# A decoder kernel on one Trainium2 core: two fetch pointers for the expert tiles, gates multiplied in before the next tile, a sum moved from GpSimd to VectorE, and one comparison instruction for two

## The chip, the cores and the metric

The kernel runs on one core of one Trainium2 chip. The core's engines are TensorE (PE in the profile, its weight loads PEld), VectorE (DVE), ScalarE (ACT), GpSimd (POOL) and SyncE (SP), which here only issues DMA transfers; 16 DMA engines move data between HBM and the on-chip memory. The metric is the device time of one execution in microseconds. A difference of about 0.3% (5 us here) is what a measurement of this kernel can tell from no change.

## The reference, cut to what matters

Two layers over 256 positions of 1024 features. Each layer is an attention (latent attention in layer 0, a sparse one in layer 1) followed by a feed-forward part of 16,384 small experts, "PEER", of which every token takes 16 for each of 8 heads. The change lies in that second part:

```python
def chunk(xc):                                     # 128 tokens
    q = (xc @ w_q).reshape(128, 8, 2, 128)
    sc = jnp.einsum("thpd,hpnd->thpn", q, subkeys)
    s_half, i_half = lax.top_k(sc, 16)             # per half, of 128 keys
    cand = s_half[:, :, 0, :, None] + s_half[:, :, 1, None, :]
    best, pos = lax.top_k(cand.reshape(128, 8, 256), 16)
    experts = ...                                  # i * 128 + j of the 16 best pairs
    g = jax.nn.softmax(best, axis=-1)
    a = gelu(einsum("thkd,td->thk", u[experts], xc))
    return einsum("thk,thkd->td", g * a, v[experts])
```

u and v are two tables of 16,384 rows of 1024 floats, 64 MB each per layer.

## The kernel before, in words

**Dense instead of gathered.** For 192 of the 256 tokens (`ND`) the kernel takes no rows by index. It streams the whole of u through TensorE as 128 tiles of 128 experts x 1024 (512 KB each), which gives every expert's dot product with every token; applies gelu; multiplies by a gate matrix that is zero where a token didn't choose the expert; and multiplies the result with the 128 tiles of v. The other 64 tokens are served by gathered rows: GpSimd fetches rows of u and v by index, and VectorE does the dot products (`g_dot`, L525) and the weighted sums (L537).

**The stages of a layer.** Attention; 16 tiles of the routing projection `p_wq` with the scores and the top-16 searches on VectorE; the u tiles (`u_step`); the v tiles. In the profiled execution the u tiles run from 178 to 541 us in layer 0 and from 1064 to 1430 us in layer 1.

**Split and plain tiles.** All weights are one list, `self.stream`, fetched in order by SP. A split tile comes into one of four places (`raw`). ScalarE rounds it to `hi` (L146), VectorE computes `lo = raw - hi` (L160), and `u_step` multiplies both with the activations, which are held as `hT` in the same two parts: 16 matmuls of `hi` and `lo` against them. Of each layer's 128 u tiles 75 are plain (`natural(j)`: every second one up to tile 44, two of three from there, none of the last four). They need neither ScalarE nor VectorE: they are loaded as `nat` and multiplied as full float32 with `xF`, the sum of the two parts of the activations, which L543 computes on GpSimd as the peer part begins.

**The fetch order.** `_sdma` (from L103) walks the list with one pointer, `sd`. A split tile is issued if it is no further than `_ahead()` says (as many split tiles as there are places); a plain one if it is at most `LEADN` = 4 tiles ahead of the tile in use, else the walk stops there, and what follows in the list waits too. `_slo` calls it after each `lo`, `end()` after each tile's matmuls. SP runs its queue in order: a `nat` transfer waits until TensorE is done with the tile that held its buffer, a `raw` one until its place is free. `nxt()` hands out the next tile: `prep()` (the `lo` of this tile, two `hi` ahead, the next `lo`), then `tick()`, which runs the functions put off by `defer(n, ...)`, n tiles later.

**The gates.** `final_gen` leaves, per token, the indices (`selI`) and the gates (`selG`) of its choices. For a group of 4 tokens (the quad, 48 of them per layer) `g_gen` has VectorE compare the indices against a ramp, once for each index part (L676, L677: 512 elements each, float16, so each choice becomes a one-hot row), and multiply one of the two by the gates in two parts (L678, L679). When two quads lie ready, `g_flush(2)` issues 8 one-hot matmuls for each (`acc<-hot`), which leave in PSUM the gate of every expert for 4 tokens. For slots of `A` that gelu has already filled, VectorE multiplies the gates in (L702); into the others ScalarE copies them (L704).

**The loop over the u tiles** (from L835) for tile j: `u_step(j)`, the matmuls; `u_fin` of tile j-1, which multiplies the gelu of the tile before it into its slot (L794), adds the two halves of a split tile (L803) and starts its gelu on ScalarE (L805, L808); `g_flush(2)`; `run_side`, which spends a budget of 0.8 (`GB`, in estimated us) on VectorE's side work, among it `g_gen`; and the dot products of gathered rows that are due. The engines take their instructions in the order in which they are written.

**After the last u tile** `w_start` turns the first slots into the weights `W` of the v stage (L819, L824), and the v tiles follow in the same list, as pairs of 1 MB.

Of the kernel before, what the change touches and what calls it, by code (L numbers as in the profile page):

```python
# [12 lines left out]
F32 = mybir.dt.float32  # L13
F32R = mybir.dt.float32r
BF16 = mybir.dt.bfloat16
F16 = mybir.dt.float16
# [31 lines left out]
class Kern:  # L48
# [5 lines left out]
    def plan(self):  # L54
        I, L = self.I, []
        self.v0s, self.spare, self.pairs = [], None, {}
        self.nh, self.odd, self.nat, self.natural = 0, {}, set(), {}
        if "mla" in self.parts:
            L += [I["a_w_in"][k] for k in range(KC)]
            L += [I["a_wk"][i] for i in range(2)]  # L60
            L += [I["a_wq"][i] for i in range(3)]
            L += [I["a_wv"][i] for i in range(2)]
            L += [I["a_wq"][i] for i in range(3, 6)]
            L += [I["a_wo"][i] for i in range(KC)]
        for l in (0, 1):
            if l == 1 and "nsa" in self.parts:
                L += [I["s_wv"][i] for i in range(4)]
                L += [I["s_wT"][i] for i in range(4)]
                L += [I["b_wg"]]
                L += [I["s_wT"][i] for i in range(4, 8)]  # L70
                L += [I["b_wq"][i] for i in range(4)]
                L += [I["b_wq"][i] for i in range(4, 8)]
                L += [I["b_wo"][i] for i in range(KC)] + [I["b_wo"][i] for i in range(KC // 2)]
            if f"peer{l}" in self.parts:
                L += [I["p_wq"][l, i] for i in range(16)]
                self.nat.update(len(L) + j for j in range(P) if natural(j))
                self.odd.update((len(L) + j, 0) for j in range(P))
                L += [I["p_u"][l, (P - FIRST + j) % P] for j in range(P)]
                self.v0s.append(len(L))
                o = (len(L) - len(self.nat) - self.v0s[0] + sum(i < self.v0s[0] for i in self.nat)) % 4  # L80
                self.odd.update((len(L) + j, 1) for j in range(P))
                self.pairs.update((len(L) + j, I["p_v"][l, j:j + 2].rearrange("j i d -> i j d")) for j in range(o % 2, P - 1, 2))
                L += [I["p_v"][l, j] for j in range(P)]
        self.stream = L
        self.v0 = self.vb = self.v0s[0]
        self.rank = [0]
        for i in range(len(L) + 1):
            self.rank.append(self.rank[-1] + (i not in self.nat))
        self.si = 0
        self.used = 0  # L90
        self.sd = 0
        self.sh = 0
        self.sl = 0
        self.raws, self.his, self.los = {}, {}, {}
        self.share = False
        self.alt = {}
        self.later, self.now = [], 0
# [5 lines left out]
    def _sdma(self, upto, now=False):  # L103

        while self.sd <= min(upto, len(self.stream) - 1):
            i, ap = self.sd, self.stream[self.sd]
            if i in self.nat:
                if i > self.used + LEADN:
                    return
                self.natural[i] = self.shl.tile([P, D], F32, tag="lo", name="nat")  # L110
                self.nc.sync.dma_start(self.natural[i], ap)
                self.sd += 1
                continue
            n, k, q = ap.shape[-1], self.place(i), i - self.v0
            o = self.place(self.v0)
            ring = self.spare if self.spare is not None and 0 <= q < P and (q + o) % 8 > 3 else self.raw4
            if 0 <= q < P and i in self.pairs:
                if i == upto and not now:
                    return
                t = ring[:, k:k + 2]  # L120
                self.nc.sync.dma_start(t, self.pairs[i])
                self.raws[i], self.raws[i + 1] = t[:, 0], t[:, 1]
                self.sd += 2
                continue
            t = ring[:, k, 0:n]
            self.nc.sync.dma_start(t, ap)
            self.raws[i] = t
            self.sd += 1

    def _shi(self, upto):  # L130
        while self.sh <= min(upto, len(self.stream) - 1):
# [48 lines left out]
    def nxt(self, prep=True, tick=True):  # L180
        i = self.si
        self.si += 1
        self.used = max(self.used, i - 1)
        if prep:
            self.prep()
        if tick:
            self.tick()
        if i in self.nat:
            return self.natural.pop(i), None
        return self.his.pop(i), self.los.pop(i)  # L190

    def end(self):

        self.used = self.si - 1
        self._sdma(self._ahead())

    def prep(self):
        self._slo(self.si)
# [284 lines left out]
    def peer(self, l):  # L483
        tc, nc, I = self.tc, self.nc, self.I
        self.v0 = self.v0s.pop(0)
        with ExitStack() as es:
# [8 lines left out]
                        return x[:, j - j0, :]  # L495

            sel = pool(es, "select")
            selI = sel.tile([P, 2, S], F16, name="selI")
            selG = sel.tile([P, 2, S], F16, name="selG")

            gat = pool(es, "gather")
# [17 lines left out]
            def g_x():  # L519
                for hh in range(2):  # L520
                    nc.gpsimd.dma_start(gacc[hh * GT:hh * GT + GT], self.hD[P - GT:P, 1, :])
# [18 lines left out]
            rt = pool(es_r, "route")  # L540
            oh = lambda sh, dt, name: rt.tile(sh, dt, tag="oh", name=name, bufs=8)
            xhi, xlo = self.hT
            nc.gpsimd.tensor_tensor(xF, xhi[:, :, 0:ND].bitcast(F32), xlo[:, :, 0:ND].bitcast(F32), op=OP.add)  # L543
            subT = rt.tile([P, 8, 2, P], F32, name="subT")
            def load_sub(h):
                nc.gpsimd.dma_start(subT[:, h], I["p_sub"][l, h])
# [49 lines left out]
            def final_gen(tt):  # L596
# [61 lines left out]
                for w in range(3):  # L658
                    self.tr(ps[:, w * P:(w + 1) * P], sel[:, w, :])
                ts = slice(tt * P, (tt + 1) * P)  # L660
                nc.vector.tensor_copy(selI[:, :, ts], ps[:, 0:256].rearrange("p (a b) -> p a b", a=2)); yield 0.35

                nc.vector.tensor_scalar(selG[:, 0, ts], ps[:, 256:384], GS, None, op0=OP.mult); yield 0.25
                nc.vector.scalar_tensor_tensor(selG[:, 1, ts], ps[:, 256:384], GS, selG[:, 0, ts],
# [2 lines left out]
            def g_gen(hot):  # L667

                b4 = [P, 2, P, 2]
                for t0 in range(0, ND, 4):  # L670
                    while len(gq) == 2:
                        yield None
                    oi, oj, gh = (hot[:, t0 // 4 % 2, a] for a in range(3))
                    bc = lambda x: x[:, t0:t0 + 4].rearrange("p (g s) -> p g s", s=2)[:, :, None, :].to_broadcast(b4)
                    tt = nc.vector.tensor_tensor
                    tt(oj, self.iota4, bc(selI[:, 1, :]), op=OP.is_equal); yield 0.34  # L676
                    tt(oi, self.iota4, bc(selI[:, 0, :]), op=OP.is_equal); yield 0.34  # L677
                    tt(gh, oj, bc(selG[:, 0, :]), op=OP.mult); yield 0.34  # L678
                    tt(oj, oj, bc(selG[:, 1, :]), op=OP.mult)  # L679
                    gq.append((t0, oi, (gh, oj)))  # L680
                    yield 0.34
# [88 lines left out]
            def u_step(j):  # L770
                hi, lo = self.nxt()
                ps = self.ps()
                if lo is None:
                    for k in range(KC):
                        self.mm(ps[:, 0:ND], hi[:, k * P:(k + 1) * P], xF[:, k, :], k == 0, k == KC - 1)
                else:

                    def high(k):
                        self.mm(ps[:, 0:2 * ND], hi[:, k * P:(k + 1) * P], self.hTT[:, k, :, 0:ND], k == 0, k == KC - 1)

                    for k in range(KC - 1):
                        high(k)
                    for k in range(KC):
                        self.mm(ps[:, 0:ND], lo[:, k * P:(k + 1) * P], xhi[:, k, 0:ND], False, False)
                    high(KC - 1)
                self.end()
                return j, ps, lo is not None
# [47 lines left out]
            for j in range(P):  # L835
                if j == 5:
                    g_x()
                x = u_step(j)
                u_fin(pu)
                pu = x  # L840
                g_flush(2)
                run_side(1.8 if len(A) == 1 else GB)
                if not side and len(A) == 1:
                    es_r.close()

                    dj = j + 2
                    hot = self.pr8.tile([P, 2, 3, 2, P, 2], F16, tag="r8", name="hot")
                    A.append((self.pr8.tile([P, NEXT, ND], F32, tag="r8", name="A2"), 0, NEXT))
                    n = P - FIRST - NEXT
                    A.append((pool(es_1, "slots1").tile([P, n, ND], F32, name="A1"), NEXT, n))  # L850
                    side.append(g_gen(hot))
                while dj and dc < P // 2 and j >= dj + int((P - 4 - dj) / 64 * dc):
                    g_dot(dc)
                    dc += 1
                    if dc == P // 2:
                        g_weights()
                if done["g"] == ND and j >= P - 3 and not W:
                    w_start()
# [860 lines left out]
```

## Time and profile before

| | |
|---|---|
| median of 3 runs | 1739.75 us (1735.94 to 1739.81) |
| the profiled execution | 1736.79 us |
| its span, first to last instruction | 1734.9 us |
| mean granted TensorE clock | 0.979 |
| TensorE busy | 1655.4 us |
| VectorE busy | 1500.6 us |
| ScalarE busy | 844.6 us |
| GpSimd busy | 493.7 us |
| moved by DMA | 476 MB, 274 GB/s on average |

The span leaves out 1.9 us of the profiled execution's own time. All durations below are from that one execution. TensorE's busy time covers matmuls that run at a reduced clock too; the granted clock says which. A row of a group ends in the idle time that its engine spent directly before it, and in what ended that idle time.

### The profile page before, as it was taken

What the parts mean: (1) busy time and instruction counts of PE and PEld (TensorE: products, weight loads), DVE (VectorE), ACT (ScalarE), POOL (GpSimd) and SP (SyncE); (2) the same over time, 40 slices, a digit from 0 to 9 for tenths busy, and PEclk for the clock granted to TensorE, in tenths of its full rate; (3) what the DMA queues carried; (4) which work ended last, traced back from release to release, by engine and by line L of the source; (5) the groups of instructions that cost most, each with busy time, mean ns of one, the idle gap of its engine ahead of it and who ended that gap; (6) DMA issues with size and microseconds to landing.
All of it is one profiled execution on the core that took longest, in us unless ns stands there. A gap on an engine that the chain in (4) does not pass through costs nothing.

```text
span 1734.9 us, 28555 instructions
## 1 busy us (share of the span) xinstructions
PE 1655.4 (95%) x9954; PEld 1484.7 (86%) x9954; DVE 1500.6 (86%) x3671; ACT 844.6 (49%) x1805; POOL 493.7 (28%) x382
## 2 busy tenths in 40 slices
PE   8998999999998999999998989998999999999997
PEld 7768998999997888888886779998999887888886
DVE  6786998899897999999777777997889879999998
ACT  6644443333325555556456744443333335555554
POOL 2020003323232543440431220022222226643420
PEclk9999999999999999999997999999999999999999
DMA  7525669798888999998572354678898898999992
GB/s 252 176 84 184 219 212 334 276 326 310 309 313 307 402 352 354 358 366 293 193 241 73 107 194 160 217 253 305 317 314 317 284 334 322 400 354 362 345 363 98
DMA packets 130142, 476.21 MB, mean 274 GB/s; under 512 B 12976, under 2 KB 15056, under 8 KB 128912
## 3 DMA queue, kind: packets, MB, share of 16 engines
q1 hardware_dynamic: 88960, 322.60, 52.3%
q0 software_dynamic: 41040, 151.80, 24.5%
q8 instruction: 79, 1.29, 0.3%
q14 instruction: 63, 0.52, 0.1%
HBM read 468.58 MB, written 5.24 MB: 273 GB/s over the span
## 4 chain that ended last, share of the span: by engine, by line
PE 64%; DVE 18%; DMA 12%; ACT 4%; issue 2%; POOL 0%; SPq 0%; ACTq 0%
PE acc L236 39%; PE mm L236 23%; DMA raw<-p_u 9%; DVE lo L160 4%; ACT hi L146 2%; DVE row L525 2%; PE mm L263 1%; DMA raw<-p_wq 1%; DVE A L702 1%; DVE idx L567 1%; DMA raw<-p_v 1%; DVE mm L803 1%; DVE vals L565 1%; DMA row<-p_ur,gidx 1%; DVE hot L676 0%
## 5 line engine op out<-in xcount | busy, mean ns | idle before, releaser
L146 ACT CAST hi<-raw 128x1024 fp32r<-128x1024 f32 (+1 forms) x315 | 328.2, 1045 | 356.5 <-DMA raw<-p_u 192.0
L160 DVE TENSOR_TENSOR lo<-raw,hi 128x1024 fp32r<-128x1024 f32 (+1 forms) x311 | 386.7, 1248 | 65.2 <-ACT hi L146 57.9
L236 PE MATMUL acc<-hi,W 128*128 128x512 f32 x1452 | 411.2, 392 | 5.7 <-ACT W L819 5.7
L236 PE MATMUL mm<-xF,nat 128*128 128x192 f32 x2400 | 410.4, 327 | 2.1 <-DVE hot L679 1.3
L236 PEld LDWEIGHTS mm<-xF,nat 128*128 128x128 f32 x2400 | 391.8, 190 | 3.8 <-issue 3.5
L516 POOL DMA_INDIRECT row<-p_v,gidx x128 | 244.9, 1913 | 317.0 <-DVE gacc L537 231.9
L236 PEld LDWEIGHTS acc<-hi,W 128*128 128x128 f32 x1452 | 274.4, 189 | 63.5 <-ACT W L819 6.2
L516 POOL DMA_INDIRECT row<-p_ur,gidx x128 | 152.8, 1194 | 578.2 <-DVE A L794 191.4
L236 PE MATMUL acc<-lo,W 128*128 128x512 f32 x968 | 300.7, 392 | 3.0 <-DVE lo L160 3.0
L236 PE MATMUL mm<-hT,hi 128*128 128x384 f32 (+1 forms) x1504 | 288.2, 329 | 14.5 <-DVE A L794 14.3
L236 PEld LDWEIGHTS mm<-hT,hi 128*128 128x128 f32 x1504 | 234.0, 195 | 20.6 <-issue 16.9
L236 PEld LDWEIGHTS acc<-lo,W 128*128 128x128 f32 x968 | 182.9, 189 | 42.8 <-DVE lo L160 4.7
L146 ACT CAST hi<-spare 128x1024 fp32r<-128x1024 f32 x120 | 126.1, 1051 | 108.3 <-PE acc L236 108.3
L537 DVE SCALAR_TENSOR_TENSOR gacc<-row,ggate,gacc 128x1024 f32<-128x1024 f32 x126 | 161.3, 1280 | 0.0
L525 DVE SCALAR_TENSOR_TENSOR row<-row,gacc 128x1024 f32<-128x1024 f32 x128 | 156.1, 1219 | 2.5 <-DMA row<-p_ur,gidx 2.5
L236 PE MATMUL mm<-hT,lo 128*128 128x192 f32 (+1 forms) x1176 | 157.6, 277 | 0.1
L160 DVE TENSOR_TENSOR lo<-spare,hi 128x1024 fp32r<-128x1024 f32 x120 | 146.6, 1222 | 9.9 <-ACT hi L146 9.8
L236 PEld LDWEIGHTS mm<-hT,lo 128*128 128x128 f32 x1176 | 154.1, 194 | 0.6 <-DVE lo L160 0.5
L824 DVE TENSOR_TENSOR W<-A,W 128x128 fp32r<-128x128 f32 (+1 forms) x512 | 107.9, 253 | 1.3 <-ACT W L819 1.3
L808 ACT ACTIVATE A<-mm 128x192 f32<-128x192 f32 (+23 forms) x236 | 62.1, 277 | 76.7 <-DVE mm L803 69.3
L805 ACT ACTIVATE mm<-mm 128x192 f32<-128x192 f32 (+23 forms) x178 | 43.9, 247 | 113.2 <-DVE mm L803 112.6
L702 DVE SCALAR_TENSOR_TENSOR A<-acc,A 128x176 f32<-128x176 f32 (+10 forms) x260 | 55.1, 271 | 38.5 <-ACT A L808 26.8
(278 smaller groups left out, 1827.0 us busy)
## 6 DMA issues: line engine op xcount, KB each, us to landing
nat<-p_u SPq DMA_DIRECT2D x150, 512.0 KB, 5.1
raw<-p_v SPq DMA_DIRECT2D x65, 1024.0 KB, 8.5
spare<-p_v SPq DMA_DIRECT2D x63, 1024.0 KB, 8.8
raw<-p_u SPq DMA_DIRECT2D x106, 512.0 KB, 5.7
raw<-p_wq SPq DMA_DIRECT2D x32, 512.0 KB, 3.8
raw<-b_wo SPq DMA_DIRECT2D x12, 512.0 KB, 3.6
raw<-a_wo SPq DMA_DIRECT2D x8, 512.0 KB, 4.7
raw<-s_wT SPq DMA_DIRECT2D x8, 512.0 KB, 4.2
```

What stands on the lines that cost most here:

```text
L146: self.nc.scalar.copy(self.his[i], self.raws[i])
L160: e.tensor_tensor(self.los[i], raw, self.his[i].bitcast(F32), op=OP.subtract)
L236: self.nc.tensor.matmul(out, a, b, start=start, stop=stop)
L263: self.nc.tensor.transpose(out, in_, self.ident[:n, :n])
L516: nc.gpsimd.indirect_dma_start(out=t, out_offset=None, in_=gtable[c // (P // 2)], in_offset=bass.IndirectOffsetOnAxis(ap=gidx[:, cc:cc + 1 ...
L525: nc.vector.scalar_tensor_tensor(t, t, 1.0, gacc, op0=OP.mult, op1=OP.mult, accum_out=gdot[:, c:c + 1])
L537: nc.vector.scalar_tensor_tensor(gacc, t, ggate[:, c:c + 1], gacc, op0=OP.mult, op1=OP.add)
L565: nc.vector.max(out=v[:, c], in_=s); yield 0.19
L702: nc.vector.scalar_tensor_tensor(y, pv[:, j0:j0 + m], 1.0 / GS, y, op0=OP.mult, op1=OP.mult)
L805: nc.scalar.activation(ps[:, 0:n], ps[:, 0:n], AF.Gelu)
L808: nc.scalar.activation(y[:, n:ND], ps[:, n:ND], AF.Gelu)
L824: nc.vector.tensor_tensor(WW[j][:, o:o + c.stop - c.start], slot(j)[:, c], WW[j][:, c].bitcast(F32), op=OP.subtract)
```

## The change

Four edits.

1. **Two pointers.** `_sdma` passes over plain tiles; a new `_snat` with its own pointer `sn` issues them up to `LEADN` tiles ahead of the tile in use. `nxt()` calls it as it begins, `end()` calls it in place of `_sdma`. So a split tile no longer waits in the list behind a plain one.
2. **The flush comes first.** `g_flush(2)` stands before `u_step(j)`: the one-hot matmuls and the multiplication of the gates come ahead of tile j's matmuls and its `lo`, no longer behind.
3. **`xF` later and elsewhere.** The sum of the two parts of the activations is put off by 8 tiles of the routing projection and done by VectorE.
4. **One comparison.** `selI` is stored so that both index parts of a quad lie side by side, and one instruction of 1024 elements makes both one-hot tables. The estimated cost of a quad falls from 1.36 to 1.28, so that the side work makes two quads ready every 3.2 tiles and not every 3.4.

```diff
@@ _sdma
             if i in self.nat:
-                if i > self.used + LEADN:
-                    return
-                self.natural[i] = self.shl.tile([P, D], F32, tag="lo", name="nat")
-                self.nc.sync.dma_start(self.natural[i], ap)
                 self.sd += 1
                 continue
...
+    def _snat(self):
+
+        while self.sn <= min(self.used + LEADN, len(self.stream) - 1):
+            i = self.sn
+            self.sn += 1
+            if i in self.nat:
+                self.natural[i] = self.shl.tile([P, D], F32, tag="lo", name="nat")
+                self.nc.sync.dma_start(self.natural[i], self.stream[i])
@@ nxt
         self.used = max(self.used, i - 1)
+        self._snat()
         if prep:
@@ end
         self.used = self.si - 1
-        self._sdma(self._ahead())
+        self._snat()
@@ peer
-            selI = sel.tile([P, 2, S], F16, name="selI")
+            selI = sel.tile([P, S // 4, 2, 4], F16, name="selI")
...
-            nc.gpsimd.tensor_tensor(xF, xhi[:, :, 0:ND].bitcast(F32), xlo[:, :, 0:ND].bitcast(F32), op=OP.add)
+            self.defer(8, lambda: nc.vector.tensor_tensor(xF, xhi[:, :, 0:ND].bitcast(F32), xlo[:, :, 0:ND].bitcast(F32), op=OP.add))
@@ g_gen
-                    tt(oj, self.iota4, bc(selI[:, 1, :]), op=OP.is_equal); yield 0.34
-                    tt(oi, self.iota4, bc(selI[:, 0, :]), op=OP.is_equal); yield 0.34
+                    tt(h[:, 0:2].rearrange("p w g i s -> p (w g) i s"), self.iota4[:, 0, None].to_broadcast([P, 4, P, 2]),
+                       selI[:, t0 // 4].rearrange("p w (g s) -> p (w g) s", s=2)[:, :, None, :].to_broadcast([P, 4, P, 2]),
+                       op=OP.is_equal); yield 0.6
                     tt(gh, oj, bc(selG[:, 0, :]), op=OP.mult); yield 0.34
@@ the loop over the u tiles
+                g_flush(2)
                 x = u_step(j)
                 u_fin(pu)
                 pu = x
-                g_flush(2)
                 run_side(1.8 if len(A) == 1 else GB)
```

What this does to the order in which the engines get their work, at three places. `raw` is a split tile, `nat` a plain one, `p_wq` the routing weights, `p_u` and `p_v` the tables.

SP's queue where the u tiles of layer 0 begin, before:

```order
L126 DMA raw<-p_wq 128x1024 x16
L111 DMA nat<-p_u 128x1024
L126 DMA raw<-p_u 128x1024
L111 DMA nat<-p_u 128x1024
L126 DMA raw<-p_u 128x1024
L111 DMA nat<-p_u 128x1024
```

and now:

```order
L123 DMA raw<-p_wq 128x1024 x16
L123 DMA raw<-p_u 128x1024 x3
L134 DMA nat<-p_u 128x1024
L123 DMA raw<-p_u 128x1024
L134 DMA nat<-p_u 128x1024
L123 DMA raw<-p_u 128x1024
```

Three split tiles are asked for before the first plain one; from there both orders alternate, and the split tile that stands beside a plain one is a later one of the list than it was.

SP's queue at the end of the same stage, before:

```order
L126 DMA raw<-p_u 128x1024
L111 DMA nat<-p_u 128x1024 x2
L126 DMA raw<-p_u 128x1024
L111 DMA nat<-p_u 128x1024
L126 DMA raw<-p_u 128x1024 x4
L121 DMA raw<-p_v 128x2x1024 x2
```

and now:

```order
L134 DMA nat<-p_u 128x1024 x2
L123 DMA raw<-p_u 128x1024
L134 DMA nat<-p_u 128x1024 x2
L123 DMA raw<-p_u 128x1024
L118 DMA raw<-p_v 128x2x1024 x2
```

The four split tiles that stood together behind the last plain one have moved up; one is left ahead of the first tiles of v.

VectorE's order around a flush in the later part of the u tiles of layer 0, before (`row` is a gathered row's dot product, `hot` a one-hot table, `A` the slots; L794 is the gelu multiplied into its slot, L803 the sum of a split tile's halves, L702 the gates):

```order
L794 TENSOR_TENSOR A_2978<-A_2978,mm 128x48
L679 TENSOR_TENSOR hot<-hot,selG 128x512
L525 SCALAR_TENSOR_TENSOR row,gdot<-row,gacc 128x1024
L160 TENSOR_TENSOR lo<-raw,hi 128x1024
L794 TENSOR_TENSOR A_2978<-A_2978,mm 128x48
L803 TENSOR_TENSOR mm<-mm,half 128x192
L702 SCALAR_TENSOR_TENSOR A_1338<-acc,A_1338 128x44x4
L702 SCALAR_TENSOR_TENSOR A_2974<-acc,A_2974 128x10x4
```

and now (L689 is the last `hot`, L712 the gates, L804 the gelu):

```order
L166 TENSOR_TENSOR lo<-raw,hi 128x1024
L804 TENSOR_TENSOR A_2980<-A_2980,mm 128x48
L813 TENSOR_TENSOR mm<-mm,half 128x192
L688 TENSOR_TENSOR hot<-hot,selG 128x512
L689 TENSOR_TENSOR hot<-hot,selG 128x512
L712 SCALAR_TENSOR_TENSOR A_1338<-acc,A_1338 128x44x4
L712 SCALAR_TENSOR_TENSOR A_2976<-acc,A_2976 128x10x4
```

Between the last `hot` of a group and the gates that come of it stood the work of one tile (at most a dot product, a `lo`, a gelu and a sum); now there is nothing, or one dot product.

More of the change, by code (lines that the diff above doesn't have):

```diff
@@ L91, in plan @@
         self.sd = 0
+        self.sn = 0
         self.sh = 0
@@ L660, in final_gen @@
                 ts = slice(tt * P, (tt + 1) * P)
-                nc.vector.tensor_copy(selI[:, :, ts], ps[:, 0:256].rearrange("p (a b) -> p a b", a=2)); yield 0.35
+                nc.vector.tensor_copy(selI[:, 32 * tt:32 * tt + 32].rearrange("p g w b -> p w g b"),
+                                      ps[:, 0:256].rearrange("p (w g b) -> p w g b", w=2, b=4)); yield 0.35
                 nc.vector.tensor_scalar(selG[:, 0, ts], ps[:, 256:384], GS, None, op0=OP.mult); yield 0.25
@@ L672, in g_gen @@
                         yield None
-                    oi, oj, gh = (hot[:, t0 // 4 % 2, a] for a in range(3))
+                    h = hot[:, t0 // 4 % 2]
+                    oi, oj, gh = (h[:, a] for a in range(3))
                     bc = lambda x: x[:, t0:t0 + 4].rearrange("p (g s) -> p g s", s=2)[:, :, None, :].to_broadcast(b4)
                     tt = nc.vector.tensor_tensor
-                    tt(oj, self.iota4, bc(selI[:, 1, :]), op=OP.is_equal); yield 0.34
-                    tt(oi, self.iota4, bc(selI[:, 0, :]), op=OP.is_equal); yield 0.34
+                    tt(h[:, 0:2].rearrange("p w g i s -> p (w g) i s"), self.iota4[:, 0, None].to_broadcast([P, 4, P, 2]),
+                       selI[:, t0 // 4].rearrange("p w (g s) -> p (w g) s", s=2)[:, :, None, :].to_broadcast([P, 4, P, 2]),
+                       op=OP.is_equal); yield 0.6
                     tt(gh, oj, bc(selG[:, 0, :]), op=OP.mult); yield 0.34
```

## The prediction

> **What bounds the kernel now.** I read the engines' sums and the chain on the profile's page first, then the windows by stage, then TensorE's groups in the u tiles, then the waits.
>
> ```profile
> PE 1655.4 (95%) x9954; PEld 1484.7 (86%) x9954; DVE 1500.6 (86%) x3671; ACT 844.6 (49%) x1805; POOL 493.7 (28%) x382
> PE acc L236 39%; PE mm L236 23%; DMA raw<-p_u 9%; DVE lo L160 4%; ACT hi L146 2%; DVE row L525 2%; PE mm L263 1%; DMA raw<-p_wq 1%; DVE A L702 1%; DVE idx L567 1%; DMA raw<-p_v 1%; DVE mm L803 1%; DVE vals L565 1%; DMA row<-p_ur,gidx 1%; DV
> ```
>
> TensorE is busy for 95% of the span and carries most of the chain; the first thing on it that isn't a matmul is the transfer of split u tiles, 9%. The columns of the windows are start and end, length, busy time of PE, PEld, DVE, ACT and POOL, granted clock, DMA share, GB/s.
>
> ```profile
> 178.00:285.00 107.00, 106.85 (x712) 106.35 (x710) 99.81 (x405) 47.28 (x100) 11.89 (x10) 1.00 0.68 234
> 285.00:344.00 59.00, 52.95 (x371) 51.56 (x371) 45.54 (x124) 20.19 (x69) 15.97 (x14) 0.94 0.84 307
> 344.00:430.00 86.00, 84.68 (x626) 82.95 (x625) 78.43 (x219) 31.60 (x98) 24.77 (x22) 1.00 0.90 320
> 430.00:530.00 100.00, 95.64 (x683) 93.55 (x682) 88.70 (x228) 33.47 (x104) 32.00 (x26) 0.98 0.89 314
> 530.00:545.00 15.00, 10.64 (x63) 9.40 (x63) 7.86 (x17) 6.86 (x16) 0.00 (x0) 0.88 0.87 307
> 545.00:833.00 288.00, 288.00 (x1267) 238.19 (x1266) 275.20 (x462) 169.86 (x263) 112.66 (x60) 0.99 0.91 338
> 1172.00:1425.00 253.00, 238.97 (x1715) 233.81 (x1716) 217.18 (x577) 87.17 (x275) 72.08 (x62) 0.98 0.88 311
> 1425.00:1440.00 15.00, 10.74 (x40) 7.97 (x39) 7.43 (x18) 7.74 (x17) 0.00 (x0) 0.77 0.78 284
> ```
>
> The v stage is full (288.00 of 288) and the first u tiles too (106.85 of 107). What can be won lies in the later u tiles and in the passage to v. In the u tiles from 285 TensorE idles 6.05 + 1.32 + 4.36 = 11.7 us, in layer 1 14.0. On top come stretches at half clock: 59 x 0.06 + 100 x 0.02 + 253 x 0.02 = 10.6 us of lost speed. Together 36 us.
>
> Who ends these gaps? First PE's row, then the engines behind it, in one gap:
>
> ```profile
> 458.73 6.20 SPq L111 DMA_DIRECT2D nat<-p_u  x2
> 462.98 1.04 ACT L146 CAST hi<-raw 128x1024 fp32r<-128x1024 f32 x1 [4.13 <-DMA raw<-p_u]
> 464.48 0.97 DVE L702 SCALAR_TENSOR_TENSOR A<-acc,A 128x188 f32<-128x188 f32 x4 [2.54 <-ACT A L808]
> 464.97 0.42 SPq L126 DMA_DIRECT2D raw<-p_u  x1
> 469.55 2.32 PE L236 MATMUL mm<-hT,hi 128*128 128x384 f32 x7 [2.39 <-DVE A L794]
> ACT hi L146 <- DMA raw<-p_u: 91.0, 39, 5.6
> ```
>
> Read it upward. TensorE waited 2.39 us for VectorE; VectorE had waited 2.54 us in L702 for a gelu; that gelu stood on ScalarE behind a cast which waited 4.13 us for its split tile. SyncE meanwhile sat 6.20 us in front of two plain tiles, the next split one behind them. ScalarE loses 91 us to such waits between 178 and 543 us.
>
> **Two pointers.** 7 matmuls took 2.32 us after that gap; the usual row, further down, has 1.52. A late split tile so costs idle time and clock. The change lets split tiles be asked for up to four split tiles ahead, held only by the `lo` that frees their place. A transfer's median time to landing is
>
> ```profile
> nat<-p_u SPq DMA_DIRECT2D x50, 512.0 KB, 5.4
> raw<-p_u SPq DMA_DIRECT2D x29, 512.0 KB, 6.7
> ```
>
> and a split tile comes every three tiles there, about 8.5 us (the flush rows below are 8.45 apart), so a tile asked for three split tiles ahead has over 20 us for its 6.7. Of the 36 us I take back 60%, -22: not all, since part of the gaps begin on VectorE itself. Bounds: 0 and -36.
>
> **The passage to v.** TensorE idles 4.36 us in the window 530 to 545 and 4.26 in 1425 to 1440, and the clock costs 15 x 0.12 + 15 x 0.23 = 5.3: 14 us.
>
> ```profile
> 514.18 9.37 SPq L126 DMA_DIRECT2D raw<-p_u  x4
> 530.68 3.13 SPq L121 DMA_DIRECT2D raw<-p_v  x2
> 538.80 1.04 ACT L146 CAST hi<-raw 128x1024 fp32r<-128x1024 f32 x1 [6.44 <-DMA raw<-p_v]
> 541.12 0.89 PE L236 MATMUL acc<-hi,W 128*128 128x512 f32 x2 [3.32 <-ACT W L819]
> ```
>
> The last four split tiles are issued together from 514.18, behind the last plain one; the first pair of v needs the places of two of them, is asked for at 530.68, and ScalarE, which has to cast it before it makes `W`, waits 6.44 us. Asked for earlier, these four are cast and freed earlier. I take -11; bounds 0 and -14.
>
> **xF off GpSimd.**
>
> ```profile
> 121.05 4.42 POOL L543 TENSOR_TENSOR xF<-hT 128x1536 f32<-128x1536 f32 x1 [6.67 <-DVE hT L347]
> L160 DVE TENSOR_TENSOR lo<-raw,hi x2: 1218/2876/4535, 120.9 to 122.0; 128x1024 fp32r<-128x1024 f32 x2
> L160 DVE TENSOR_TENSOR lo<-raw,hi 128x1024 fp32r<-128x1024 f32 x10 | 12.2, 1222 | 2.6 <-ACT hi L146 2.4
> 119.00:141.00 22.00, 15.71 (x97) 13.14 (x96) 12.80 (x10) 8.46 (x15) 10.23 (x12) 0.95 0.70 247
> 141.00:178.00 37.00, 36.99 (x301) 36.80 (x301) 29.31 (x135) 17.00 (x34) 0.00 (x0) 0.94 0.48 139
> ```
>
> While GpSimd added, one `lo` took 4.54 us in place of 1.22: 3.3 us on a stretch where TensorE idles 6.3 of 22. That is -3.3 per layer, -6.6. The Trainium skill ("SBUF — State Buffer", Who interferes with whom) says that a VectorE instruction with two SBUF inputs and a GpSimd instruction that reads SBUF lock each other out for a whole instruction; the trace agrees, with 4.54 against 1.22. On VectorE the sum of 1536 elements costs 1.22 x 1.5 = 1.8 us, between routing tiles where VectorE is busy 29.31 of 37 us: hidden; if not, +1.8 per layer. Bounds 0 and -6.6.
>
> **One comparison.** The rows below show two comparisons starting 0.33 us apart.
>
> ```profile
> 433.13 0.41 DVE L676 TENSOR_TENSOR hot<-iota,selI 128x512 f16<-128x512 f16 x1
> 433.46 0.42 DVE L677 TENSOR_TENSOR hot<-iota,selI 128x512 f16<-128x512 f16 x1
> ```
>
> One of 1024 elements saves at most one start, about 0.09 (0.42 long, 0.33 apart): 0.58 to 0.67 us for two at 0.67. At the speed of `lo` (1024 float32 elements) it would take 1.22. I take 0.60, nearest the same type: 96 quads x 0.07 = -6.7 us of VectorE, which isn't the bound on average: 0 on the path.
>
> **The flush a tile earlier.** This speaks against the change. Its cost depends on when the tables are ready.
>
> ```profile
> 418.25 2.76 PE L236 MATMUL mm<-xF,nat 128*128 128x192 f32 x16
> 420.08 0.42 DVE L679 TENSOR_TENSOR hot<-hot,selG 128x512 f16<-128x512 f16 x1
> 412.40 1.08 PE L236 MATMUL acc<-hot 128*128 128x128 f16 x16
> 420.85 1.08 PE L236 MATMUL acc<-hot 128*128 128x128 f16 x16
> 424.29 1.52 PE L236 MATMUL mm<-hT,hi 128*128 128x384 f32 x7
> L677 DVE TENSOR_TENSOR hot<-iota,selI 128x512 f16<-128x512 f16 x18 | 7.5, 419 | 0.0
> L702 DVE SCALAR_TENSOR_TENSOR A<-acc,A 128x176 f32<-128x176 f32 (+10 forms) x54 | 10.3, 251 | 4.6 <-ACT A L808 4.3 <-PE acc L236 0.4
> L794 DVE TENSOR_TENSOR A<-A,mm 128x64 f32<-128x64 f32 (+9 forms) x30 | 7.1, 235 | 0.0
> ```
>
> The last table is ready at 420.50. TensorE takes the flush at 420.85, after the two plain tiles that begin at 418.25; moved ahead of the last of them it would be wanted one tile (2.8 us at most) earlier. VectorE then has to be faster than TensorE within the loop: tables, one-hot matmuls, gates, next tables. From 344 to 430 there are 30 tiles (L794) and 9 flushes (18 quads). VectorE: quads 9 x 2 x 1.34 = 24.1, gates 10.3, the rest 44.0, or 1.47 per tile. With the change a flush with 3.2 tiles costs 2 x 1.27 + 1.14 + 3.2 x 1.47 = 8.4 us of VectorE; TensorE needs 3.2 x (84.68 - 9 x 1.08) / 30 + 1.08 = 9.1. So VectorE keeps up on average, with 0.7 to spare; with three tiles between two flushes it is 8.1 against 8.6. What it waits for the one-hot matmuls (1.08) can eat this reserve, unless a dot product lies there. But L702 waits less: now for the gelu two tiles back, and of 4.6 us of idle time ahead of it 4.3 were ScalarE's. I take 0.25 us a flush between 0 and 2.2 (a whole wait from the tile's start, 418.25, to 420.50): 48 x 0.25 = +12.
>
> **The sum.** 1736.8 - 22 - 11 - 6.6 + 12 = 1709, against the profiled execution; the runs' median is 3 us above it. I say 1711.
>
> **The rivals.**
>
> *Ready too late.* Each flush waits the time from the tile's start to the tables, 1.7 us as a mean if VectorE stays as it was against TensorE: 48 x 1.7 = +82, so 1736.8 - 39.6 + 82 = 1779. It becomes slower than before beyond 39.6 / 48 = 0.83 us a flush. For: VectorE is busy 78.43 of 86. Against: the reserve above. The Trainium skill ("TensorE: Matmul & The Clock Gate", Part 1: The HAM clock gate) halves the clock only after an idle window of about 3.4 us; the trace has half speed after 2.39, so short waits could cost more than that rule says. 14%.
>
> *Plain tiles late.* In SyncE's queue a plain tile now stands behind a split one that waits for a `lo`. A plain tile asked for four ahead has 4 x 2.8 = 11 us at most, less the wait for its buffer and the `lo` in front, for 5.4 us of landing at a DMA share of 0.90. If each of some 54 groups from tile 44 on loses 0.5 us: +27 in place of the -22, so 1736.8 - 6.6 - 11 + 27 = 1746. 8%.
>
> *A slow comparison.* At 1.22 us VectorE gets 96 x 0.55 = 53 us more; from 285 to 530 it has 32.3 us idle, and 35.8 in layer 1, so that 26 each all but fill it. With half of it on the path 1709 + 27 = 1736, no change. For: a new form with two broadcast operands that no row shows. 10%.
>
> *The gaps are VectorE's.* The casts come earlier but VectorE's own row of work sets the pace (88.70 of 100): the 22 stay, the flush costs nothing new: 1736.8 - 6.6 - 11 = 1719, with part of the 11 lost up to 1728. 18%.
>
> **How the numbers follow.** The forecast has 50%: 1711, on its own 1692 (half the flush's cost, and 36 for 22) to 1725. The cases at 1719 to 1746 have 36%; so 1690 to 1746 leaves out the late tables and half the far ends, less than 2 in 10. What a measurement can tell from no change is 5 us: faster 0.50 + 0.18 + a little of the slow comparison = 0.70; same, most of the slow comparison and some of the late plain tiles, 0.10; slower 0.20.
>
> **What would show it.** Two pointers right: ScalarE's waits for `raw<-p_u` fall from 91 us to below 40, and PE's busy share from 430 to 530 rises above 97 of 100. Passage: ScalarE's 6.44 before the first pair of v is gone. xF: no `lo` above 1.3 us near 122. Comparison: a row of 0.6 to 0.8 us with 1024 elements. The flush: the idle time ahead of `acc<-hot` sums to about 12 us over both layers; above 40 the forecast is wrong and the first rival holds. If the waits for `raw` stay, the order on SyncE was not the cause.

## The result, and the profile after

The changed kernel takes 1694.87 us as the median of 4 runs (1692.29 to 1697.03), the kernel before 1739.65 us (1735.94 to 1739.81): a ratio of 0.9747, 95% interval 0.9728 to 0.9766. It is 45 us faster. Three single executions that were slow (two of the run a_ptr below, at 2345 and 9380 us, and one of the kernel before, at 1754.55 us) are left out of all numbers here. The span of the profiled execution fell from 1734.9 to 1693.2 us, by 41.7.

The engines' sums and the chain, from the page of the changed kernel:

```profile
span 1693.2 us, 28432 instructions
PE 1634.7 (97%) x9954; PEld 1471.0 (87%) x9954; DVE 1492.8 (88%) x3575; ACT 846.2 (50%) x1795; POOL 504.9 (30%) x380
PE acc L243 40%; PE mm L243 31%; DMA nat<-p_u 3%; DVE lo L166 2%; DMA raw<-p_v 1%; PE mm L270 1%; DMA row<-p_ur,gidx 1%; DVE row L532 1%; ACT hi L152 1%; DMA raw<-p_wq 1%; DMA xT<-xT 0%; DMA bounce<-ropeO 0%; DMA raw<-a_w_in 0%; DVE bnst L3
```

The split u tiles' transfer, 9% of the chain before, is gone from it; plain tiles have 3%. TensorE does the same 9954 matmuls in 20.7 us less (1655.4 to 1634.7) and idles 21.0 us less (79.5 to 58.5). Half of the gain is thus matmuls that run at full clock again: the mean granted clock rose from 0.979 to 0.991, and busy time times clock comes out nearly the same (1620.6 and 1620.0 us).

The windows by stage, first the kernel before, then the changed one; routing, u tiles and the first 20 us of v, for layer 0 and then for layer 1:

```profile
119.00:178.00 59.00, 52.70 (x396) 49.93 (x395) 42.12 (x145) 25.47 (x47) 10.23 (x12) 0.94 0.56 179
178.00:541.00 363.00, 347.92 (x2439) 341.96 (x2437) 316.52 (x980) 136.25 (x380) 84.64 (x71) 0.99 0.82 290
541.00:561.00 20.00, 18.84 (x70) 14.88 (x71) 18.97 (x38) 13.15 (x26) 8.61 (x3) 0.83 0.82 291
1010.00:1065.00 55.00, 50.48 (x383) 48.34 (x382) 39.82 (x142) 24.95 (x46) 9.55 (x12) 0.94 0.58 192
1065.00:1429.00 364.00, 347.71 (x2438) 341.76 (x2437) 317.15 (x981) 136.03 (x379) 84.14 (x71) 0.99 0.82 288
1429.00:1449.00 20.00, 17.78 (x64) 13.70 (x65) 16.06 (x32) 12.88 (x25) 4.81 (x3) 0.83 0.71 259
```

```profile
119.00:172.50 53.50, 51.69 (x405) 49.11 (x404) 41.37 (x145) 25.79 (x48) 3.31 (x7) 1.00 0.72 230
172.50:520.00 347.50, 342.91 (x2439) 339.88 (x2438) 316.93 (x940) 138.67 (x378) 87.88 (x71) 1.00 0.83 297
520.00:540.00 20.00, 19.58 (x88) 15.93 (x87) 18.94 (x35) 13.74 (x25) 9.48 (x4) 1.00 0.93 334
985.00:1038.00 53.00, 50.11 (x390) 48.02 (x389) 38.91 (x141) 24.74 (x47) 1.36 (x3) 0.97 0.69 212
1038.00:1386.60 348.60, 341.99 (x2439) 338.37 (x2438) 317.33 (x941) 138.59 (x378) 87.55 (x71) 1.00 0.84 296
1386.60:1406.60 20.00, 15.95 (x62) 12.48 (x62) 15.63 (x30) 10.58 (x21) 5.75 (x3) 0.91 0.77 280
```

The u tiles, with the gap behind them, take 15.5 and 15.4 us less. VectorE's busy time in them is the same (316.5 and 316.9 us): it wasn't relieved, but TensorE waits less for it. In 20 us of early v TensorE now gets 88 matmuls done and not 70 in layer 0, but 62 and not 64 in layer 1.

What TensorE still waits for in the u tiles and in early v, first from the changed kernel's list of waits (sum, times, longest), then two rows of its timeline (the second flush of layer 0, and the early v tiles of layer 1):

```profile
PE mm L243 <- DMA nat<-p_u: 4.3, 6, 1.5
PE acc L243 <- DVE hot L688: 4.1, 2, 2.2
PE acc L243 <- DVE hot L689: 0.5, 2, 0.2
```

```profile
279.52 0.22 PE L243 MATMUL acc<-hot 128*128 128x128 f16 x1 [1.89 <-DVE hot L688]
1396.06 0.72 PE L243 MATMUL acc<-lo,W 128*128 128x512 f32 x2 [4.05 <-DVE lo L166]
```

The one-hot matmuls wait 4.6 us in all, 4.1 of it in one wait per layer, at its second flush. A wait of 4.05 us in early v of layer 1 is larger than before.

Of the marks set in the prediction: ScalarE's waits for split u tiles (91 us a layer) no longer stand in the list of waits; TensorE is busy 342.91 of 347.50 us, 98.7%, over all u tiles of layer 0; the 6.44 us before the first pair of v are not gone but 4.48 in layer 0 and 4.93 in layer 1, now while TensorE is still busy with the last u tiles, and all waits of ScalarE for v rose from 10.6 to 16.1 us; the comparison takes 0.69 us; no `lo` in layer 0's routing takes over 1.3 us. The flush's waits are 4.6 us, where 12 were forecast.

### The profile page after: what moved, and what is told of

The parts are those of the page before. It is cut to its first block, busy times and chain, and to the rows that moved or that the text cites. A ratio compares the mean times of both kernels' runs of the same rounds, so it can differ in the third digit from the quotient of the medians.

```text
span 1693.2 us, 28432 instructions
## 1 busy us (share of the span) xinstructions
PE 1634.7 (97%) x9954; PEld 1471.0 (87%) x9954; DVE 1492.8 (88%) x3575; ACT 846.2 (50%) x1795; POOL 504.9 (30%) x380
## 4 chain that ended last, share of the span: by engine, by line
PE 73%; issue 9%; DVE 8%; DMA 7%; ACT 3%; SPq 0%; POOL 0%; DVEq 0%; ACTq 0%; POOLq 0%
PE acc L243 40%; PE mm L243 31%; DMA nat<-p_u 3%; DVE lo L166 2%; DMA raw<-p_v 1%; PE mm L270 1%; DMA row<-p_ur,gidx 1%; DVE row L532 1%; ACT hi L152 1%; DMA raw<-p_wq 1%; DMA xT<-xT 0%; DMA bounce<-ropeO 0%; DMA raw<-a_w_in 0%; DVE bnst L317 0%; ACT p L1610 0%
## 5 line engine op out<-in xcount | busy, mean ns | idle before, releaser
L166 DVE TENSOR_TENSOR lo<-raw,hi 128x1024 fp32r<-128x1024 f32 (+1 forms) x311 | 381.4, 1231 | 65.1 <-ACT hi L152 32.3
L523 POOL DMA_INDIRECT row<-p_v,gidx x128 | 260.8, 2037 | 292.6 <-DVE gacc L544 216.5
L523 POOL DMA_INDIRECT row<-p_ur,gidx x128 | 156.4, 1222 | 569.5 <-DVE row L532 165.7
L243 PE MATMUL mm<-hT,hi 128*128 128x384 f32 (+1 forms) x1504 | 280.4, 322 | 0.0
L243 PEld LDWEIGHTS mm<-hT,hi 128*128 128x128 f32 x1504 | 227.3, 189 | 1.9 <-issue 1.2
L243 PE MATMUL mm<-hT,lo 128*128 128x192 f32 (+1 forms) x1176 | 154.0, 273 | 0.0
L243 PEld LDWEIGHTS mm<-hT,lo 128*128 128x128 f32 x1176 | 150.5, 190 | 0.0
L818 ACT ACTIVATE A<-mm 128x192 f32<-128x192 f32 (+18 forms) x224 | 60.0, 278 | 83.5 <-DVE mm L813 71.5
L714 ACT ACTIVATE A<-acc 128x24 f32<-128x24 f32 (+22 forms) x124 | 34.7, 308 | 131.2 <-DVE A L712 111.1
```

Source lines behind the costliest of these rows:

```text
L166: e.tensor_tensor(self.los[i], raw, self.his[i].bitcast(F32), op=OP.subtract)
L243: self.nc.tensor.matmul(out, a, b, start=start, stop=stop)
L523: nc.gpsimd.indirect_dma_start(out=t, out_offset=None, in_=gtable[c // (P // 2)], in_offset=bass.IndirectOffsetOnAxis(ap=gidx[:, cc:cc + 1 ...
L714: nc.scalar.activation(x[:, m:n, t0:t0 + 4], pv[:, j0 + m:j0 + n], AF.Copy, scale=1.0 / GS)
L818: nc.scalar.activation(y[:, n:ND], ps[:, n:ND], AF.Gelu)
```

## The experiments

Two families: the changed kernel with one edit undone, and the kernel before with one edit alone; then versions in which split tiles are asked for less far ahead. Each line of results has the ratio to the kernel before on the same chip, since chips differ by some us. *Theory A* was the prediction's: late split tiles cause the gaps. *Rival B*: the early flush itself removes them. *Rival C*: VectorE has less to do.

**u_ptr: one pointer again.**

```diff
@@ _sdma
+                if i > self.used + LEADN:
+                    return
+                self.natural[i] = ...
+                self.nc.sync.dma_start(self.natural[i], ap)
...
-    def _snat(self): ...
@@ end
-        self._snat()
+        self._sdma(self._ahead())
```

> The changed kernel with one fetch pointer again; the other three edits stay. Theory A (late split tiles on ScalarE cause the gaps of the u tiles and of the passage to v; two pointers remove them): about 32 of the 45 us come back, 1722 to 1732, ScalarE's waits for split u tiles return to about 90 us a layer. Rival B (the gates no longer stand behind a gelu that stands behind a cast, so the earlier flush removes the gaps): 1700 to 1708, the waits for split tiles return but TensorE's gaps stay small. Rival C (VectorE's time): as B.

Measured: 1740.34 us, ratio 1.0013 (0.9981 to 1.0044). All of the gain is gone, more than theory A said. The waits of ScalarE and TensorE, first in the kernel before, then in u_ptr:

```profile
ACT hi L146 <- DMA raw<-p_u: 192.0, 81, 5.6
PE mm L236 <- DVE A L794: 14.7, 14, 3.5
PE acc L236 <- DVE hot L678: 6.1, 2, 3.1
PE acc L236 <- DVE hot L679: 3.0, 7, 1.1
```

```profile
ACT hi L146 <- DMA raw<-p_u: 190.1, 77, 6.0
PE acc L236 <- DVE hot L682: 22.5, 30, 2.7
PE acc L236 <- DVE hot L681: 14.9, 16, 2.7
```

The waits for split tiles are back at 190 us over both layers, and TensorE's gaps moved to the one-hot matmuls: 37.4 us there against 9.1 before, while the 14.7 us in front of the tiles' own matmuls (L794) are down to 0.3. Rivals B and C fall: three edits without the pointers gain nothing. The prediction's rival of tables that come too late is real with one pointer; with two, these waits are 4.6 us.

**a_flush: the early flush alone on the kernel before.**

```diff
+                g_flush(2)
                 x = u_step(j)
                 u_fin(pu)
                 pu = x
-                g_flush(2)
```

> The kernel before with the early flush alone. By u_ptr (1740 with xF's 5 to 8 us in it) it is slower than before: 1743 to 1750, with some 35 us of TensorE idle in front of the one-hot matmuls. Rival B: 1715 to 1725.

Measured: 1744.36 us, ratio 1.0063 (1.0040 to 1.0086), a little slower. The waits:

```profile
ACT hi L146 <- DMA raw<-p_u: 189.0, 74, 6.6
PE acc L236 <- DVE hot L679: 24.8, 36, 2.3
PE acc L236 <- DVE hot L678: 12.8, 15, 3.1
```

The same picture without the other edits. By itself this edit costs 0.6%, 11 us.

**u_flush: the flush behind the tile, the other edits kept.** The edit is the reverse of the last.

> The changed kernel with the flush behind the tile again. Theory A: within 5 us of 1695, or slightly faster, since the flush a tile earlier costs between 0 and 0.25 us each. Rival B: 1710 to 1720. If the flush's cost that I predicted (12 us) was paid and covered by a larger gain elsewhere: 1683.

Measured: 1705.07 us, ratio 0.9845 (0.9783 to 0.9907). Theory A said within 5 us of 1695, and missed: beside two pointers the early flush gains. On the same chip u_cmp (below), which keeps it, ran at 1689.90 to 1693.01 us, u_flush at 1702.35 to 1715.21. TensorE waits here for something else, by the waits and by one place in the timeline (VectorE, SyncE, TensorE in order of time):

```profile
PE mm L243 <- DMA nat<-p_u: 17.5, 18, 3.9
DVE A L712 <- PE acc L243: 32.2, 24, 6.2
```

```profile
329.44 1.22 DVE L166 TENSOR_TENSOR lo<-raw,hi 128x1024 fp32r<-128x1024 f32 x1
330.69 0.33 SPq L123 DMA_DIRECT2D raw<-p_u  x1
331.11 1.36 SPq L134 DMA_DIRECT2D nat<-p_u  x2
338.81 0.40 PE L243 MATMUL mm<-xF,nat 128*128 128x192 f32 x1 [0.85 <-DMA nat<-p_u]
```

SyncE can ask for the split tile only when the `lo` that frees its place ends (330.66); two plain tiles stand behind it, are asked for from 331.11, and TensorE waits for one 0.85 us at 338.81. VectorE does that `lo` late where it stands in L712 for the one-hot matmuls: 32.2 us of waiting, against 16.0 in the changed kernel. This is a ring, since the one-hot matmuls are late where TensorE waited for a plain tile, and the trace doesn't say where it begins. The next test takes SyncE out of it: a split tile that never waits there.

**three_late: the flush behind the tile, split u tiles three ahead.** With four places and three tiles ahead, the place is free when the transfer is asked for.

```diff
-        while n + 1 < len(self.stream) and self.rank[n + 2] - self.rank[self.sl] <= self.nraw:
+        lim = self.nraw - (v0 - P <= self.sl < v0 - 6)
+        while n + 1 < len(self.stream) and self.rank[n + 2] - self.rank[self.sl] <= lim:
...
-                g_flush(2)
                 x = u_step(j)
                 u_fin(pu)
                 pu = x
+                g_flush(2)
```

> The changed kernel with the flush behind the tile, and split u tiles asked for three split tiles ahead and not four, so that none waits on SyncE for a lo that is still to come and no plain tile stands behind such a wait. If the order on SyncE is what the early flush mends: the 16.3 us that TensorE idles for plain tiles in u_flush fall below 5 and the time from 1705 to about 1694. Rival D (the early flush gains in itself, by gates that wait less on VectorE): 1705 as before.

Measured: 1684.97 us, ratio 0.9729 (0.9699 to 0.9760): 20 us less than u_flush and faster than forecast. SyncE's waits between 260 and 520 us in u_flush, in the changed kernel and in three_late (a split tile's transfer that waits for VectorE is put down there to the `lo` or to the gelu that follows it); after them two waits of the whole of three_late, and its windows of the u tiles:

```profile
SPq L123 <- DVE A L804: 104.4, 18, 7.8
SPq L123 <- DVE lo L166: 74.8, 13, 7.5
SPq L134 <- PE mm L243: 37.6, 28, 3.3
```

```profile
SPq L123 <- DVE A L804: 81.2, 20, 5.8
SPq L134 <- PE mm L243: 77.4, 41, 3.3
SPq L123 <- DVE lo L166: 47.4, 11, 6.1
```

```profile
SPq L134 <- PE mm L244: 184.8, 53, 5.6
SPq L123 <- DVE lo L166: 12.1, 3, 5.2
SPq L123 <- DVE A L805: 3.2, 3, 2.7
```

```profile
DVE A L713 <- PE acc L244: 13.3, 22, 1.8
PE mm L244 <- DMA nat<-p_u: 2.1, 2, 1.5
```

```profile
171.00:514.50 343.50, 341.33 (x2442) 338.52 (x2441) 317.17 (x943) 135.78 (x378) 90.55 (x71) 1.00 0.86 302
1031.00:1374.00 343.00, 341.07 (x2439) 338.15 (x2438) 316.82 (x942) 135.76 (x377) 91.14 (x71) 1.00 0.86 302
```

By these rows SyncE waited 179 us for VectorE in front of split tiles in u_flush, 129 in the changed kernel, 15 here; what it waits for now is a plain tile's buffer, 184.8 us. TensorE's wait for plain tiles fell from 17.5 to 2.1 us, and it is busy 341.3 of 343.5 us. VectorE's wait for the one-hot matmuls fell to 13.3 us although the flush still stands behind the tile: most of the 32.2 came with the late plain tiles.

**three: the same, with the early flush.**

```diff
-        while n + 1 < len(self.stream) and self.rank[n + 2] - self.rank[self.sl] <= self.nraw:
+        lim = self.nraw - (v0 - P <= self.sl < v0 - 6)
+        while n + 1 < len(self.stream) and self.rank[n + 2] - self.rank[self.sl] <= lim:
```

> The changed kernel with split u tiles asked for three split tiles ahead. If the order on SyncE costs it the 4.3 us of waits for plain tiles: 1690 to 1692. If one place less makes split tiles late again: 1700 or more, with ScalarE waiting for them.

Measured: 1686.67 us, ratio 0.9738 (0.9705 to 0.9771), the same as three_late within the intervals. Its interval also meets the changed kernel's (0.9728 to 0.9766), so this run doesn't show what the shorter reach is worth beside the early flush. Where no plain tile waits behind a split one, it makes no difference that can be measured where the flush stands.

**u_cmp: two comparisons again.**

```diff
...
-                    tt(h[:, 0:2]..., selI[:, t0 // 4]..., op=OP.is_equal); yield 0.6
+                    tt(oj, self.iota4, bc(selI[:, 1, :]), op=OP.is_equal); yield 0.34
+                    tt(oi, self.iota4, bc(selI[:, 0, :]), op=OP.is_equal); yield 0.34
```

> The changed kernel with two comparisons of 512 and their old cost of 0.34 each (flushes every 3.4 tiles). Theory A: within 5 us of 1695. Rival C: 1705 or more, and TensorE waits for hot tables more than the 5.0 us of the changed kernel.

Measured: 1692.52 us, ratio 0.9760 (0.9710 to 0.9810). No effect that can be measured, as theory A had it; rival C falls. The one comparison in the changed kernel's timeline:

```profile
403.30 0.69 DVE L685 TENSOR_TENSOR hot<-iota,selI 128x1024 f16<-128x1024 f16 x1
```

It takes about as long as two that start 0.33 us apart.

**u_xf: xF on GpSimd at once,** and **xf_pool_late: put off by 8 tiles, but on GpSimd.**

```diff
-            self.defer(8, lambda: nc.vector.tensor_tensor(xF, ...))
+            nc.gpsimd.tensor_tensor(xF, ...)                        # u_xf
+            self.defer(8, lambda: nc.gpsimd.tensor_tensor(xF, ...)) # xf_pool_late
```

> The changed kernel with xF on GpSimd at once. By the trace after, the gain of this edit in layer 0 is 7.3 us (the matmuls' lag against before goes from +2.1 to -5.25 between 124 and 146 us) and some 3 in layer 1: 1705. By the prediction's price of 3.3 a layer: 1701.5. If it is hidden: 1695.

> The changed kernel with xF put off by 8 tiles but still on GpSimd. If the delay is what helps (the lo that it blocks is on TensorE's path only at the layer's start): within 3 us of the changed kernel, with one lo of over 3 us at about 150 us that nobody waits for. If GpSimd's hold of VectorE costs wherever it falls: 4 to 8 us slower.

Measured: u_xf 1700.34, ratio 0.9809 (0.9754 to 0.9864); xf_pool_late 1699.06, ratio 0.9801 (0.9775 to 0.9827), 7.2 us above the changed kernel's 1691.86 beside it. The second is no test of a delay. The sum on GpSimd, in u_xf's timeline and then in xf_pool_late's:

```profile
121.84 4.42 POOL L550 TENSOR_TENSOR xF<-hT 128x1536 f32<-128x1536 f32 x1 [6.68 <-DVE hT L354]
```

```profile
121.80 4.42 POOL L550 TENSOR_TENSOR xF<-hT 128x1536 f32<-128x1536 f32 x1 [4.06 <-DVE hT L354]
```

It starts at the same moment, while in the changed kernel VectorE does it here:

```profile
144.90 1.77 DVE L550 TENSOR_TENSOR xF<-hT 128x1536 f32<-128x1536 f32 x1
```

GpSimd had nothing else to do, so the instruction that is written later started as soon as its operands were there. Whether GpSimd's hold of VectorE would hurt at a later time stays open, since no run put the sum there; nor does one do the sum on VectorE at once, so how much of this edit's gain is the engine and how much the delay isn't shown.

**a_ptr and a_ptr2: two pointers alone on the kernel before.** The edit is the change's first part; a_ptr2 is the same kernel again.

> The kernel before with the two pointers alone. Theory A: most of the gain comes with them, but with the flush behind the tile plain tiles come late behind split ones that wait for a lo (16 us of TensorE idle in u_flush): 1737 - 22 - 11 + a part of those, 1708 to 1714. Rival B (the gain needs the early flush): above 1725.

> The kernel before with two pointers alone, again, for a profile at a granted clock above 0.97: 0.986 to 0.992 of before, 1712 to 1721. TensorE idle for plain tiles 12 to 20 us over both layers, ScalarE's waits for split u tiles below 5 us.

Measured: 1707.16 to 1715.13 us in three executions, ratio 0.9893 (0.9851 to 0.9935), and 1711.90 us, ratio 0.9880 (0.9855 to 0.9905). TensorE's waits for plain tiles in a_ptr2:

```profile
PE mm L243 <- DMA nat<-p_u: 11.4, 8, 3.5
```

Alone the pointers bring 1.1 to 1.2%, 19 to 21 us, nearly half of the gain. ScalarE's waits for split u tiles are gone from the list, and plain tiles are late by 11.4 us, a little under what was expected.

**after_again and minimal.** The changed kernel as a yardstick, and what the runs pointed to: two pointers with split tiles three ahead, xF on VectorE, the flush and the comparisons as before. The diff is against the changed kernel.

```diff
+        lim = self.nraw - (v0 - P <= self.sl < v0 - 6)
...
-                    tt(h[:, 0:2]..., selI[:, t0 // 4]..., op=OP.is_equal); yield 0.6
+                    tt(oj, ...); yield 0.34
+                    tt(oi, ...); yield 0.34
...
-                g_flush(2)
                 x = u_step(j)
                 u_fin(pu)
                 pu = x
+                g_flush(2)
```

> The changed kernel itself, as the yardstick for the runs beside it: 0.975 of before, 1695.

> Two pointers with split u tiles three ahead, and xF late on VectorE; the flush behind the tile and two comparisons, as before. If neither the early flush nor the one comparison is worth anything once no plain tile waits behind a split one: 1682 to 1688, faster than the changed kernel by 7 to 12 us. If one of them counts: 1690 or more, with TensorE idle in front of plain tiles or of one-hot matmuls.

Measured side by side: after_again 1691.86 us, ratio 0.9767 (0.9740 to 0.9794); minimal 1685.31 us (1684.51 to 1687.17), ratio 0.9728 (0.9702 to 0.9755). The ranges of single runs don't overlap (1690.85 to 1694.59 for after_again). Two of the four edits with a shorter reach beat the four without it by 6.5 us; all four with it (three, 0.9738) are no faster than the two.

## Why the prediction was right, and where it wasn't

The time lies in the range and the direction was right, but the gain was 45 us where 29 were forecast, and 1694.87 is near the lower end of the range. By TensorE's timeline, from the first to the last matmul of the u tiles and from there to the 41st of v, the 41.7 us of the span come from the u tiles (12.1 and 13.3 us in the two layers), the passage to v (6.9 and 1.6) and the stretch up to each layer's first u tile (5.3 and 2.7). The prediction had -22 + 12 = -10, -11 and -6.6 for them. The passage and xF came near their size in sum; the miss is in the u tiles, 25 us for 10, and there in the sign of the flush. Point by point:

- **Two pointers (-22 in the u tiles, -11 in the passage).** Cause right: with one pointer all of the gain is gone and the waits for split tiles are back. Alone they bring 19 to 21 us and not 33, because the rival of late plain tiles, which I gave 8%, held in part (11.4 us of waits in a_ptr2, 17.5 in u_flush). In minimal, with split tiles three ahead, these waits are 3.7 us, and its 2.7% less 7 us for xF leaves about 40 us for the pointers and the reach together. So the term's condition was missing: that no plain tile stands on SyncE behind a split one that has to wait.
- **The flush a tile earlier (+12).** This step failed as the prediction put it. I priced it by VectorE's speed against TensorE's, on the trace of before, and added it to the pointers' gain as if the two were independent. With one pointer it costs about what I said, 11 us in a_flush, but by luck: the 12 us were to be idle time in front of the one-hot matmuls, and that is 37.6 us there against 9.1 before, while the 14.7 us in front of the tiles' own matmuls fell to 0.2. With two pointers the tables are late mainly at each layer's second flush (4.1 of 4.6 us), and the edit gains 0.8 to 1.0% against u_flush (the single runs don't overlap, 1690.85 to 1697.03 against 1702.35 to 1715.21). That it gains by SyncE's queue is shown from two sides: SyncE's waits for VectorE in front of split tiles are 179 us with the flush behind the tile and 129 with it ahead, and with the wait taken off SyncE it is worth nothing that can be measured (0.9738 against 0.9729). The sign is set by what stands on SyncE, which my term didn't contain. The prediction also took the row at 418.25 for two plain tiles; its 16 matmuls are one, and the bounds stay as they are.
- **xF (-6.6).** Right in sum: 7.2 us against xf_pool_late; by the timeline 5.3 us in layer 0 and 2.7 in layer 1, where 3.3 each were reckoned. The Trainium skill ("SBUF — State Buffer", Who interferes with whom) has the mutual lock; the trace of the kernel before agrees, with 4.54 us for a `lo` of 1.22. On VectorE the sum took 1.77 us, where 1.8 was reckoned.
- **One comparison (0 on the path).** Right: 0.69 us for 1024 elements against 0.42 for 512, which start 0.33 apart, and no effect on the time that can be measured.
- **The clock.** I counted 10.6 us for it in the u tiles and 5.3 in the passage. TensorE's whole busy time fell by 20.7 us with the same matmuls. The routing stages ran at 0.94 before and at 1.00 and 0.97 after; I left those out.

**Left open.** The 4.05 us in early v of layer 1 stand in every version with two pointers (3.2 to 5.3 us). In each, ScalarE's cast just ahead waits for a pair of v, in the changed kernel here:

```profile
1389.00 0.88 SPq L118 DMA_DIRECT2D raw<-p_v  x2
1394.78 1.05 ACT L152 CAST hi<-raw 128x1024 fp32r<-128x1024 f32 x1 [3.82 <-DMA raw<-p_v]
```

The pair is asked for at 1389.00, right after the `lo` that ends at 1388.80, and the cast begins 5.8 us later. In the kernel before the cast waited 3.12 us for that pair and TensorE, which ran at a lower clock there, 1.21. No run asks for it earlier.

## What to carry to other kernels

When two edits act on one loop, price them together: ask of a wait that an edit adds who makes the waited-for thing late, and whether another edit removes that. In a queue that runs in order, a transfer asked for before its place is free holds back everything behind it (in u_flush SyncE stood so for 179 us of 260, and TensorE idled 17.5 us for the tiles behind): reach one tile less far, so that nothing in the queue waits for work that is still to come. And undo one edit at a time once the whole is faster: here two of four carried nothing measurable once the first had the right reach.

## What the runs showed of the hardware that was not expected

An instruction put off in the program is not put off in time on an idle engine: written 8 tiles later, GpSimd's sum began at 121.80 us, as it did at 121.84 when written at once.

Short gaps cost more clock than I reckoned. Behind TensorE's gap of 2.39 us at 467 us of the kernel before, its granted clock was 0.50:

```profile
470.50:472.00 1.50, 1.50 (x7) 1.50 (x6) 1.50 (x4) 1.47 (x4) 0.24 (x1) 0.50 0.76 208
```

In the same kernel, the granted clock of the routing window was 0.94 with 6.3 us of idle time in 59 (its longest gaps were 1.92 and 3.44 us); in the changed kernel it was 1.00 with 1.8 us in 53.5, so that the lost speed before (0.06 x 59, about 3.5 us) was over half as large as the idle time itself.
